# A streaming encoder trunk on one core: the first block's short rows loaded as half rows, and another order of its first casts

## The chip, the core and the metric

The kernel runs on one core of a Trainium2 chip. The time is that of the device in microseconds (us) for one execution, and the figure for a kernel is the median of its runs. Engines are named as in the profile: PE is TensorE, DVE is VectorE, ACT is ScalarE, POOL is GpSimd, and SP issues most of the transfers (DMAs).

## The reference, cut to what matters

One layer of a trunk works on 2048 prompt frames and on 32 frames of a running stream, each with 1024 channels. Everything is float32.

```python
def rmsnorm(x, g):
    y = x32 * lax.rsqrt(jnp.mean(x32 * x32, axis=-1, keepdims=True) + EPS)
    return (y * g).astype(x.dtype)

hn = rmsnorm(h, g_mix)
proj = hn @ w_in                                  # 1024 -> 3072
hA, bA, cA, zA, vB, zB = jnp.split(proj, ...)     # six bands of 512
yA = bA * (depthwise width-3 conv of cA * hA, with bias) * silu(zA)
yB = (trailing mean of vB minus vB, a linear map per group, a scale) * silu(zB)
h = h + concat[yA, yB] @ w_out
h = h + (p @ w_ple) * sigmoid(rmsnorm(h, g_ple) @ w_ple_gate)
y = rmsnorm(h, g_final)                           # also the last rows of cA*hA and vB
```

## The kernel before, in words

The frames are cut into blocks of 416 (`NB`). A block has three tiles of 128 frames and a short one of 32 rows (`DEC`). Blocks 0 and 1 form the first group. Channels lie on partitions for the products, in chunks of 128, and eight chunks make two halves of 512 channels (`NH`, `KH = 4` chunks each).

A float32 product is made of three matrix passes over numbers split in two: `hi` is the value rounded to fp32r (a cast), `lo` is the rest (a subtraction). The passes are hi·hi, hi·lo and lo·hi. `first_products` runs them for block 0 in this order for three bands at once (`zb`, `v`, `c`): the eight hi·hi matmuls of zb, of v and of c come first, then those with the frames' `lo`, then those with the weights' `lo`.

Before that, block 0 must be made ready. This is the code that is changed:

- SP loads three tiles of 128 rows (`xt_0_0`, `xt_0_1`, `xt_0_2`; below x0, x1, x2), then the short rows of blocks 0 and 1 as one tile of 64 partitions by 1024 channels (`xt_0_3`), then the raw weights of zb, v and c. SP's transfers go out in the order of its queue.
- For each tile, `x_stat` sums the squares on ACT (line 93) and makes the reciprocal root of the mean on POOL (`ms` at line 72, `rstd` at line 76). `first_normal` multiplies by it and by the gain on DVE, one half of the channels at a time (line 641). The gain lies in two PSUM banks (`gm_0`, `gm_1`, in the code `pg`).
- `first_turn` transposes on PE: four 128x128 transposes for a half of a tile, and eight 64-row transposes for the short rows (line 650). Their results are in PSUM (`pt0_0_0` is tile 0, half 0).
- `first_hi` casts from PSUM into the block's frames `B`, on ACT (one on DVE; line 663), and `first_lo` subtracts on DVE (line 667). The casts of the raw weights are at lines 694 and 712.
- `fill(n, t)` runs n transposes of the identity that nothing reads. Seven stand ahead of the first tile's transposes, then two, three and two behind those of x0, x1 and x2.

There are six PSUM banks for products (`bank`) and two others (`tbank`). The six hold `short_bank` and five of the tiles' transposes; the sixth, `pt0_2_1`, takes the bank of `pt0_0_0` when its `lo` has been made, and the first product, `zb`, takes that of `pt0_0_1`.

The order on an engine is mostly the scheduler's. What goes through `in_turn` (`tc.keep_in_program_order`) keeps the place it has in the program.

Much later the kernel loads the gate's weights with POOL's queue (line 1397). Its source is a view of four runs of 32 rows, written to a tile of 128 partitions by 512:

```python
rows = w_gate.rearrange("(q k c) n -> k q c n", q=4, k=KC)[k]
for half, t in enumerate(ts):
    ins = nc.gpsimd.dma_start(t, rows[:, :, half * NH:half * NH + NH])
```

Of the kernel before, what the change touches and what calls it, by code (L numbers as in the profile page):

```python
# [9 lines left out]
F32 = mybir.dt.float32  # L10
# [5 lines left out]
P = 128  # L16
D = 1024
# [17 lines left out]
def trunk(ctx, tc, x_p, x_s, c_conv, c_pool, p_p, p_s, g_mix, w_in, conv_w, conv_b, pool_w,  # L35
# [308 lines left out]
    with ExitStack() as s1:  # L344
# [45 lines left out]
        def fill(n, t):  # L390

            for _ in range(n):
                tc.keep_in_program_order(nc.tensor.transpose(t[:, :P], ident, ident))
# [34 lines left out]
        def turn(x, half, name, get=tbank, later=False):  # L428
            xt, n, _ = x
            pt = get(name)  # L430
            for k in range(KH):
                kk = half * KH + k
                ins = nc.tensor.transpose(pt[:, k * P:k * P + n], xt[:n, kk * P:(kk + 1) * P], ident[:n, :n])
# [167 lines left out]
        def first_products(ws):  # L601

            x = hn[0]
            out = {kind: bank(f"{kind}0_0_0") for kind in ws}
            for a, b in ((0, 0), (0, 1), (1, 0)):
                if b:
                    next(second)  # L610
                    next(second)
                for kind, w in ws.items():
                    if a:
                        if kind == "zb":
                            next(second)
                            first_los["v"]()
                        elif kind == "v":
                            first_los["c"]()
                        next(second)
                    for k in range(KC):  # L620
                        ins = nc.tensor.matmul(out[kind][:, :NB], w[k // KH][:, k % KH, a], x[k // KH][:, k % KH, b],
                                               start=a + b + k == 0, stop=a == 1 and k == KC - 1, skip_group_check=True)
                        if a + b + k or kind != "zb":
                            in_turn(ins)
# [11 lines left out]
        def first_normal(x):  # L636

            xt, m, r = x
            for half in range(2):
                h = xt[:m, half * NH:half * NH + NH]  # L640
                in_turn(nc.vector.scalar_tensor_tensor(h, h, r[:m], pg[half][:m], op0=ALU.mult, op1=ALU.mult))

        def first_turn(c, x):

            xt, m, _ = x
            if c < 3:
                return [turn(x, half, f"pt0_{c}_{half}", bank) for half in range(2)]
            t = short_bank
            for k in range(KC):
                tc.keep_in_program_order(nc.tensor.transpose(t[:, k * m:k * m + m], xt[:m, k * P:(k + 1) * P], ident[:m, :m]))  # L650
            t = t.rearrange("p (k t) -> p k t", k=KC)
            return t[:, :KH], t[:, KH:]

        first_x, turned_x = [], {}

        def place0(c, half):
            n = P if c < 3 else DEC
            piece = B0[("11", "21")[half]][:, :, :, c * P:c * P + n]
            return piece[:, :, 0], piece[:, :, 1], turned_x[c][half][:, :, :n]

        def first_hi(c, half, copy=nc.scalar.copy):
            hi, _, src = place0(c, half)
            in_turn(copy(hi, src))
# [5 lines left out]
        def first_tile(c):  # L669
            first_normal(first_x[c])  # L670
            turned_x[c] = first_turn(c, first_x[c])
            if c < 3:
                fill((2, 3, 2)[c], short_bank)


        for c in range(3):
            first_x.append(x_stat(ahead0[c], True))
        first_tile(0)
        first_hi(0, 0)
        first_x.append(x_stat(short0, True))  # L680
        short0 = first_x[3]
        first_tile(1)
        first_hi(0, 1)
        first_lo(0, 0)
        for half in range(2):
            first_hi(1, half)
        first_tile(2)
        first_hi(2, 0)
        first_tile(3)
        first_hi(2, 1, nc.vector.tensor_copy)  # L690
        raw = raw_weight("zb", 0, "firstzb")
        first_zb = [wtile(f"w_firstzb_{half}") for half in range(2)]
        for half, t in enumerate(first_zb):
            in_turn(nc.scalar.copy(t[:, :, 0], raw[:, half * KH:half * KH + KH]))
        for half in range(2):
            first_hi(3, half)
        for c in range(4):
            for half in range(2):
                if c + half:
                    first_lo(c, half)  # L700
        hn[0] = B0["11"], B0["21"]
        for half, t in enumerate(first_zb):
            nc.vector.tensor_tensor(t[:, :, 1], raw[:, half * KH:half * KH + KH], t[:, :, 0].bitcast(F32), op=ALU.subtract)
        first_w.append(first_zb)

        first_los = {}
# [13 lines left out]
            return ts  # L720

        first_w.extend(other_first(kind) for kind in ("v", "c"))
        for half in range(2):
            nc.scalar.copy(g_bc[:, half * NH:half * NH + NH], pg[half])
        B0["12"] = piece_of(seventh("B0_12"), 0)
        hn[1] = B0["12"], B0["22"]

        def second_block():

            spans = [(c, slice(c * P, min(NB, c * P + P))) for c in range(4)]  # L730
            xs = []
            for c in range(3):
                x = x_tile(f"1_{c}", [x_rows(1, c)])
                normal(x)
                xs.append((x, slice(0, P)))
                yield
            xs.append((short0, slice(DEC, 2 * DEC)))
            whole = []
            for c, cs in spans:
                x, ts = xs[c]  # L740

                turned = x[0].rearrange("p (k t) -> p k t", k=KC)[:, :, :ts.stop - ts.start]
                for half, q in enumerate(("12", "22")):
                    pt = turn(x, half, f"pt1_{c}_{half}", bank)[:, :, ts]
# [33 lines left out]
        pv = tbank("pv")  # L778
        nc.tensor.transpose(pv[:, :112], rows, ident[:112, :112])
        vec = const.tile([P, 112], F32, name="vec")  # L780
        nc.vector.tensor_copy(vec, pv[:, :112])
# [1016 lines left out]
```

## Time and profile before

| what | value |
|---|---|
| median of 3 runs | 920.51 us (919.87 to 922.76) |
| the profiled execution's own time | 922.18 us |
| its span, first to last instruction | 920.4 us |
| PE busy | 907.0 us, 99% of the span |
| DVE, ACT, POOL busy | 723.2, 482.7, 159.3 us |

The profiled execution took 1.78 us more than its span. A row of the timeline gives start, length, engine, source line, operation, output and inputs, and in brackets how long the engine was idle before and what ended that. Rows of the same kind that follow each other stand as one with a count, so the time of one is best read from the distance to the next row. A matmul's end is modelled, so its length overlaps the next one's start.

### The profile page before, as it was taken

To read this page: it belongs to the slowest core of one execution; us is meant where nothing else is said; L and a number is where in the kernel's file an instruction comes from. 1 tells how busy PE (TensorE), PEld (TensorE's weight loads), DVE (VectorE), ACT (ScalarE), POOL (GpSimd) and SP (SyncE) were. 2 spreads that over 40 slices of the span, in tenths; PEclk is the share of its full clock that TensorE was granted. 3 is DMA by queue.
4 is the path that set the end of the run, shared out by engine and by line. 5 is a ranking of instruction groups with operands and counts; after the bars stand their busy time and mean duration, and the time that the engine had idled before them with its cause. 6 is when DMAs were issued, how large, how long until landed. Compare 5 with 4: busy or idle time off the path is not lost.

```text
span 920.4 us, 13201 instructions
## 1 busy us (share of the span) xinstructions
PE 907.0 (99%) x4529; PEld 824.7 (90%) x4529; DVE 723.2 (79%) x1236; ACT 482.7 (52%) x894; POOL 159.3 (17%) x307
## 2 busy tenths in 40 slices
PE   8999999999999999999999999999999999999996
PEld 6999999999999999999999988888878878888885
DVE  6996898999576989795777579666558658889885
ACT  6744565654345555453444365444436855555554
POOL 2111222121000342310000111111113301111113
PEclk9999999999999999999999999999999999999999
DMA  8357687898945789738885468865767974576554
GB/s 247 100 141 220 170 245 230 244 282 285 416 137 172 235 231 221 231 115 303 245 243 178 146 234 278 266 218 183 237 228 230 357 262 140 206 242 231 190 201 176
DMA packets 138447, 205.12 MB, mean 223 GB/s; under 512 B 13116, under 2 KB 101724, under 8 KB 137101
## 3 DMA queue, kind: packets, MB, share of 16 engines
q1 hardware_dynamic: 117773, 139.41, 47.9%
q0 software_dynamic: 17872, 59.45, 19.6%
q10 hardware_dynamic: 2736, 5.44, 1.6%
q8 instruction: 35, 0.57, 0.3%
q14 instruction: 31, 0.25, 0.1%
HBM read 136.60 MB, written 67.64 MB: 222 GB/s over the span
## 4 chain that ended last, share of the span: by engine, by line
PE 78%; DVE 6%; DMA 3%; issue 1%; ACT 1%; POOL 0%; POOLq 0%; DVEq 0%
PE x_o L175 9%; PE x_g L175 9%; PE x_zab L593 5%; PE z_g L175 5%; PE x_zbv L593 5%; PE e L107 4%; PE z_o L175 4%; PE x_ch L593 4%; PE z_zab L593 3%; PE z_zbv L593 2%; PE z_ch L593 2%; PE y_g L175 2%; PE y_o L175 2%; PE za L593 2%; PE b L593 2%; PE h L593 1%
## 5 line engine op out<-in xcount | busy, mean ns | idle before, releaser
L80 ACT CAST y_S<-y_fS 128x512 fp32r<-128x512 f32 x32 | 19.5, 622 | 36.8 <-PE x_o L175 19.0
L175 PE MATMUL x_g<-wg_b,g_S 128*128 128x512 f32 x128 | 35.7, 390 | 0.0
L175 PE MATMUL x_o<-wo_b,y_S 128*128 128x512 f32 x128 | 35.7, 391 | 0.0
L593 PE MATMUL x_zab<-B,w_zab_S 128*128 128x416 f32 x168 | 34.2, 352 | 0.2 <-ACT V L989 0.2
L593 PE MATMUL z_zab<-B,w_zab_S 128*128 128x416 f32 x168 | 34.3, 352 | 0.0
L593 PE MATMUL x_zbv<-B,w_zbv_S 128*128 128x416 f32 x168 | 34.2, 352 | 0.0
L593 PE MATMUL z_ch<-B,w_ch_S 128*128 128x416 f32 x168 | 34.1, 352 | 0.0
L593 PE MATMUL x_ch<-B,w_ch_S 128*128 128x416 f32 x168 | 34.0, 351 | 0.0
L593 PE MATMUL z_zbv<-B,w_zbv_S 128*128 128x416 f32 x168 | 34.0, 351 | 0.0
L107 PE MATMUL e<-wq,pps 128*128 128x512 f32 x144 | 33.1, 390 | 0.0
L593 PEld LDWEIGHTS x_zab<-B,w_zab_S 128*128 128x128 f32 x168 | 31.3, 188 | 0.8 <-ACT V L989 0.5
L107 PEld LDWEIGHTS e<-wq,pps 128*128 128x128 f32 x144 | 27.0, 188 | 5.6
L593 PEld LDWEIGHTS x_ch<-B,w_ch_S 128*128 128x128 f32 x168 | 31.4, 188 | 0.3
L593 PEld LDWEIGHTS z_zbv<-B,w_zbv_S 128*128 128x128 f32 x168 | 31.4, 188 | 0.3
L593 PEld LDWEIGHTS z_ch<-B,w_ch_S 128*128 128x128 f32 x168 | 31.4, 188 | 0.3
L593 PEld LDWEIGHTS z_zab<-B,w_zab_S 128*128 128x128 f32 x168 | 31.4, 188 | 0.3
L593 PEld LDWEIGHTS x_zbv<-B,w_zbv_S 128*128 128x128 f32 x168 | 31.3, 188 | 0.4
L1343 DVE TENSOR_TENSOR c_o<-x_o,x 128x512 f32<-128x512 f32 x14 | 9.7, 691 | 26.4 <-PE x_o L175 26.4
L1566 DVE SCALAR_TENSOR_TENSOR h<-h,rstd_f,g_bc 128x1024 f32<-128x1024 f32 (+1 forms) x15 | 19.3, 1284 | 14.0 <-POOL rstd_f L76 14.0
L72 POOL TENSOR_SCALAR ms_f<-ssq_f 128x1 f32<-128x1 f32 (+1 forms) x15 | 6.6, 441 | 128.7 <-ACT junk L93 128.5
L175 PEld LDWEIGHTS x_o<-wo_b,y_S 128*128 128x128 f32 x128 | 24.0, 188 | 5.2 <-DVE c_o L1343 0.3
L175 PEld LDWEIGHTS x_g<-wg_b,g_S 128*128 128x128 f32 x128 | 24.0, 188 | 5.0
(591 smaller groups left out, 2688.5 us busy)
## 6 DMA issues: line engine op xcount, KB each, us to landing
y<-y_d SPq DMA_DIRECT2D x16, 512.0 KB, 6.7
x<-in_x_prompt_dram SPq DMA_DIRECT2D x16, 512.0 KB, 4.3
h_d<-x SPq DMA_DIRECT2D x16, 512.0 KB, 3.8
h<-h_d SPq DMA_DIRECT2D x16, 512.0 KB, 3.7
xt<-in_x_prompt_dram SPq DMA_DIRECT2D x15, 512.0 KB, 7.2
e<-e_d SPq DMA_DIRECT2D x15, 512.0 KB, 6.3
out_dram<-h POOLq DMA_DIRECT2D x14, 512.0 KB, 3.0
p_dT<-T POOLq DMA_DIRECT2D x12, 512.0 KB, 6.0
```

Source lines behind the costliest of these rows:

```text
L72: nc.gpsimd.tensor_scalar(ms[:n], ssq[:n], scalar1=1.0 / D, scalar2=EPS, op0=ALU.mult, op1=ALU.add)
L80: ins = nc.scalar.copy(hi, src)
L107: nc.tensor.matmul(ps, pps[:, a, k], wp[k][b][:, cs], start=k + q == 0, stop=k == 1 and q == 2)
L175: nc.tensor.matmul(ps[:n], lhs[:, k, a, :n], w[b][:, k], start=start and k + q == 0, stop=k == KH - 1 and q == 2, skip_group_check=True)
L593: nc.tensor.matmul(ps[:, :NB], lhs[:, k, x], b[:, k, y], start=start and k + q == 0, stop=stop and k == KH - 1 and q == 2, skip_group_chec ...
L1343: add = lambda o, a, b: nc.vector.tensor_tensor(o, a, b, op=ALU.add)
L1566: nc.vector.scalar_tensor_tensor(h[:n], h[:n], rf[:n], g_bc[:n], op0=ALU.mult, op1=ALU.mult)
```

## The change

It concerns the beginning alone, up to the first products of block 0.

- The short rows of blocks 0 and 1 (64 rows) lie as half rows on 128 partitions: partitions 0 to 63 have channels 0 to 511, partitions 64 to 127 have channels 512 to 1023. Two loads bring them, one a half. The source of each is a view of two runs of 32 rows (block, row, channel), the target 64 partitions by 512.
- These two loads now stand ahead of that of x2.
- Each partition has the squares of half a row. A product with the 0/1 matrix `pair` adds the two halves, into one column of `short_bank`. `pair` is made by two additions on DVE at the start. The mean then comes from DVE (`ms_short`, line 673) and the root from POOL.
- The fills behind the tiles (2, 3 and 2) are gone. The seven at the start stay.
- The transposes of all tiles are now pinned in the order of the program. `pt0_2_1` lies in the bank of `gm_0`, so `gm_0` is copied early to `g_bc`, and `zb` takes the bank of `pt0_0_0`.
- Casts and transposes go by halves of the channels, in an order written out by hand: short half 0, x2, short half 1, and the weights' casts between those of the frames.
- The transpose of the small vectors (`pv`) moves to a place behind the first eight matmuls of c.

The diff, cut to its core:

```diff
         short_bank = bank("pt0_3")
         fill(7, short_bank)
+        HP = P // 2
+        pair = one.tile([P, P], F32, name="pair")
+        for h in range(2):
+            nc.vector.tensor_tensor(pair[:, h * HP:h * HP + HP], ident[:, :HP], ident[:, HP:], op=ALU.add)
...
-        ahead0 = [x_load(f"0_{c}", [x_rows(0, c)]) for c in range(3)]
-        short0 = x_load("0_3", [x_rows(0, 3), x_rows(1, 3)])
+        ahead0 = [x_load(f"0_{c}", [x_rows(0, c)]) for c in range(2)]
+        short_x = ring4(xin, "xt_short")
+        for h in range(2):
+            nc.sync.dma_start(short_x[h * HP:h * HP + HP, :NH],
+                              x_p[:2 * NB, h * NH:h * NH + NH].rearrange("(b n) d -> b n d", b=2)[:, 3 * P:])
+        ahead0.append(x_load("0_2", [x_rows(0, 2)]))
...
+        def short_sums():
+            ssq = sm.tile([P, 1], F32, tag="ssq", name="ssq_short")
+            in_turn(nc.scalar.activation(junk[:, :NH], short_x[:, :NH], AF.Square, accum_out=ssq))
+            return ssq
+        def short_root(ssq):
+            in_turn(nc.tensor.matmul(short_bank[:, :1], pair, ssq, start=True, stop=True))
+            ms, r = (sm.tile([P, 1], F32, tag=t, name=f"{t}_short") for t in ("ms", "rstd"))
+            in_turn(nc.vector.tensor_scalar(ms, short_bank[:, :1], scalar1=1.0 / D, scalar2=EPS, op0=ALU.mult, op1=ALU.add))
+            nc.gpsimd.tensor_tensor(r, ms, nhalf, op=ALU.pow)
+            return r
+        def short_half(half, r):
+            hs = slice(half * HP, half * HP + HP)
+            h = short_x[hs, :NH]
+            in_turn(nc.vector.scalar_tensor_tensor(h, h, r[hs], pg[half][hs], op0=ALU.mult, op1=ALU.mult))
+            n = KH * HP
+            turned_x[3, half] = short_turn(half, short_bank[:, half * n:half * n + n], in_turn)[:, :, 0]
...
-            if c < 3:
-                fill((2, 3, 2)[c], short_bank)
...
+        for c in range(2):
+            first_x.append(x_stat(ahead0[c], True))
+        short_ssq = short_sums()
+        g_copy = lambda half: nc.scalar.copy(g_bc[:, half * NH:half * NH + NH], pg[half])
+        first_tile(0)
+        in_turn(g_copy(0))
+        first_x.append(x_stat(ahead0[2], True))
+        first_normal(first_x[1], halves=(1, 0))
+        short_r = short_root(short_ssq)
+        turned_x[1] = first_turn(1, first_x[1])
+        first_hi(0, 0)
+        first_hi(1, 0)
+        short_half(0, short_r)
+        first_normal(first_x[2], (0,))
+        first_lo(0, 0)
+        first_normal(first_x[2], (1,))
+        turned_x[2] = first_turn(2, first_x[2])
+        zb_hi(0)
+        first_hi(0, 1)
+        first_hi(3, 0)
+        first_hi(2, 0)
+        short_half(1, short_r)
+        first_hi(1, 1)
+        first_hi(2, 1, nc.vector.tensor_copy)
+        zb_hi(1)
+        first_hi(3, 1)
         for half in range(2):
-            first_hi(3, half)
-        for c in range(4):
-            for half in range(2):
+            for c in range(4):
                 if c + half:
                     first_lo(c, half)
```

How it moves instructions, at three places. The first is SP's queue, from the first tile's load to the three raw weights. Before:

```order
L412 DMA xt_0_0_171<-in_x_prompt_dram 128x1024
L412 DMA xt_0_1_173<-in_x_prompt_dram 128x1024
L412 DMA xt_0_2_175<-in_x_prompt_dram 128x1024
L412 DMA xt_0_3_177<-in_x_prompt_dram 32x1024 x2
L529 DMA raw_firstzb_267<-in_w_in_dram 128x8x128
L529 DMA raw_firstv_284<-in_w_in_dram 128x8x128
L529 DMA raw_firstc_290<-in_w_in_dram 128x8x128
```

The same stretch of SP's queue in the changed kernel:

```order
L418 DMA xt_0_0_174<-in_x_prompt_dram 128x1024
L418 DMA xt_0_1_176<-in_x_prompt_dram 128x1024
L640 DMA xt_short_178<-in_x_prompt_dram 64x1x512 x2
L418 DMA xt_0_2_181<-in_x_prompt_dram 128x1024
L535 DMA raw_firstzb_186<-in_w_in_dram 128x8x128
L535 DMA raw_firstv_282<-in_w_in_dram 128x8x128
L535 DMA raw_firstc_288<-in_w_in_dram 128x8x128
```

The short rows have gone ahead of the third tile, and each of their two loads now brings 64 half rows instead of 32 whole ones.

The second place is PE, from the first tile's transposes (`pt0_0_0`, half 0) to the first matmuls of zb. Before:

```order
L433 MATMUL pt0_0_0_203<-ident_76,xt_0_0_171 128x128 x4
L433 MATMUL pt0_0_1_208<-ident_76,xt_0_0_171 128x128 x4
L393 MATMUL pt0_3_155<-ident_76 128x128 x2
L433 MATMUL pt0_1_0_224<-ident_76,xt_0_1_173 128x128 x4
L433 MATMUL pt0_1_1_229<-ident_76,xt_0_1_173 128x128 x4
L393 MATMUL pt0_3_155<-ident_76 128x128 x3
L433 MATMUL pt0_2_0_243<-ident_76,xt_0_2_175 128x128 x4
L433 MATMUL pt0_2_1_248<-ident_76,xt_0_2_175 128x128 x4
L393 MATMUL pt0_3_155<-ident_76 128x128 x2
L650 MATMUL pt0_3_155<-ident_76,xt_0_3_177 128x64 x8
L621 MATMUL zb0_0_0_321<-B0_0_180,w_firstzb_0_269 128x416 x4
L621 MATMUL zb0_0_0_321<-B0_0_180,w_firstzb_1_270 128x416 x4
```

PE in the changed kernel:

```order
L439 MATMUL pt0_0_0_206<-ident_76,xt_0_0_174 128x128 x4
L439 MATMUL pt0_0_1_211<-ident_76,xt_0_0_174 128x128 x4
L671 MATMUL pt0_3_155<-ssq_short_202,pair_163 128x1
L439 MATMUL pt0_1_0_230<-ident_76,xt_0_1_176 128x128 x4
L439 MATMUL pt0_1_1_235<-ident_76,xt_0_1_176 128x128 x4
L662 MATMUL pt0_3_155<-ident_76,xt_short_178 128x64 x4
L439 MATMUL pt0_2_0_250<-ident_76,xt_0_2_181 128x128 x4
L439 MATMUL pt0_2_1_255<-ident_76,xt_0_2_181 128x128 x4
L662 MATMUL pt0_3_155<-ident_76,xt_short_178 128x64 x4
L628 MATMUL zb0_0_0_315<-B0_0_183,w_firstzb_0_188 128x416 x4
L628 MATMUL zb0_0_0_315<-B0_0_183,w_firstzb_1_189 128x416 x4
```

The product with `pair` stands between the transposes of x0 and x1, the fills (line 393) are gone, and the short rows' transposes stand in two parts, the second one just ahead of zb.

The third place is the way to x2's and the short rows' normalisation. On POOL, from x1's root to the first one of block 1 (`x1_0`), before:

```order
L76 TENSOR_TENSOR rstd_x0_1_193<-ms_x0_1_191,nhalf_84 128x1
L72 TENSOR_SCALAR ms_x0_2_197<-ssq_x0_2_195 128x1
L76 TENSOR_TENSOR rstd_x0_2_199<-ms_x0_2_197,nhalf_84 128x1
L72 TENSOR_SCALAR ms_x0_3_218<-ssq_x0_3_216 64x1
L76 TENSOR_TENSOR rstd_x0_3_220<-ms_x0_3_218,nhalf_84 64x1
L72 TENSOR_SCALAR ms_x1_0_352<-ssq_x1_0_350 128x1
```

POOL in the changed kernel:

```order
L76 TENSOR_TENSOR rstd_x0_1_200<-ms_x0_1_198,nhalf_84 128x1
L72 TENSOR_SCALAR ms_x0_2_219<-ssq_x0_2_217 128x1
L76 TENSOR_TENSOR rstd_x0_2_221<-ms_x0_2_219,nhalf_84 128x1
L674 TENSOR_TENSOR rstd_short_227<-ms_short_226,nhalf_84 128x1
L72 TENSOR_SCALAR ms_x1_0_349<-ssq_x1_0_347 128x1
```

DVE in the changed kernel, from x1's normalisation to the first `lo` behind the cast of `pt0_2_1`:

```order
L652 SCALAR_TENSOR_TENSOR xt_0_1_176<-xt_0_1_176,rstd_x0_1_200,gm_0_151 128x512
L673 TENSOR_SCALAR ms_short_226<-pt0_3_155 128x1
L680 SCALAR_TENSOR_TENSOR xt_short_178<-xt_short_178,rstd_short_227,gm_0_151 64x512
L652 SCALAR_TENSOR_TENSOR xt_0_2_181<-xt_0_2_181,rstd_x0_2_221,gm_0_151 128x512
L698 TENSOR_TENSOR B0_0_183<-pt0_0_0_206,B0_0_183 128x4x128
L652 SCALAR_TENSOR_TENSOR xt_0_2_181<-xt_0_2_181,rstd_x0_2_221,gm_1_152 128x512
L680 SCALAR_TENSOR_TENSOR xt_short_178<-xt_short_178,rstd_short_227,gm_1_152 64x512
L694 CAST B0_0_183<-pt0_2_1_255 128x4x128
L698 TENSOR_TENSOR B0_0_183<-pt0_1_0_230,B0_0_183 128x4x128
```

On POOL the short rows' root still comes behind x2's, while on DVE the short rows' first half now comes ahead of x2's normalisation.

More of the change, by code (lines that the diff above doesn't have):

```diff
@@ L609, in first_products @@
                 if b:
+                    vectors()
                     next(second)
@@ L634, in in_turn, with first_normal @@
             tc.keep_in_program_order(ins)
-        def first_normal(x):
+        def first_normal(x, halves=(0, 1)):
             xt, m, r = x
-            for half in range(2):
+            for half in halves:
                 h = xt[:m, half * NH:half * NH + NH]
@@ L643, in first_turn, with short_turn @@
         def first_turn(c, x):
-            xt, m, _ = x
-            if c < 3:
[L647 to L652, printed above, removed]
+            gets = (bank, tbank if c == 2 else bank)
+            return [turn(x, half, f"pt0_{c}_{half}", gets[half], True) for half in range(2)]
+        def short_turn(half, t, pin=lambda ins: None):
+            hs = slice(half * HP, half * HP + HP)
+            for k in range(KH):
+                pin(nc.tensor.transpose(t[:, k * HP:k * HP + HP], short_x[hs, k * P:k * P + P], ident[hs, hs]))
+            return t.rearrange("p (k b t) -> p k b t", k=KH, b=2)
+        def short_sums():
[9 more added lines that the diff above has]
+        def short_half(half, r):
+            hs = slice(half * HP, half * HP + HP)
+            h = short_x[hs, :NH]
+            in_turn(nc.vector.scalar_tensor_tensor(h, h, r[hs], pg[half][hs], op0=ALU.mult, op1=ALU.mult))
+            n = KH * HP
+            turned_x[3, half] = short_turn(half, short_bank[:, half * n:half * n + n], in_turn)[:, :, 0]
         first_x, turned_x = [], {}
@@ L671, in first_tile, with zb_hi @@
             turned_x[c] = first_turn(c, first_x[c])
-            if c < 3:
-                fill((2, 3, 2)[c], short_bank)
[L676 to L690, printed above, removed]
         raw = raw_weight("zb", 0, "firstzb")
         first_zb = [wtile(f"w_firstzb_{half}") for half in range(2)]
-        for half, t in enumerate(first_zb):
-            in_turn(nc.scalar.copy(t[:, :, 0], raw[:, half * KH:half * KH + KH]))
+        def zb_hi(half, copy=nc.scalar.copy):
+            in_turn(copy(first_zb[half][:, :, 0], raw[:, half * KH:half * KH + KH]))
+        for c in range(2):
[24 more added lines that the diff above has]
+        first_hi(3, 1)
         for half in range(2):
-            first_hi(3, half)
-        for c in range(4):
-            for half in range(2):
+            for c in range(4):
                 if c + half:
@@ L702, in trunk @@
         for half, t in enumerate(first_zb):
-            nc.vector.tensor_tensor(t[:, :, 1], raw[:, half * KH:half * KH + KH], t[:, :, 0].bitcast(F32), op=ALU.subtract)
+            in_turn(nc.vector.tensor_tensor(t[:, :, 1], raw[:, half * KH:half * KH + KH], t[:, :, 0].bitcast(F32), op=ALU.subtract))
         first_w.append(first_zb)
@@ L722, in trunk @@
         first_w.extend(other_first(kind) for kind in ("v", "c"))
-        for half in range(2):
-            nc.scalar.copy(g_bc[:, half * NH:half * NH + NH], pg[half])
+        g_copy(1)
         B0["12"] = piece_of(seventh("B0_12"), 0)
@@ L777, in trunk, with vectors @@
         nc.sync.dma_start(rows[100:108].rearrange("k (q c) -> k q c", q=4), g_ple[0].rearrange("(q k c) -> k q c", q=4, k=KC))
-        pv = tbank("pv")
-        nc.tensor.transpose(pv[:, :112], rows, ident[:112, :112])
         vec = const.tile([P, 112], F32, name="vec")
-        nc.vector.tensor_copy(vec, pv[:, :112])
+        def vectors():
+            pv = tbank("pv")
+            nc.tensor.transpose(pv[:, :112], rows, ident[:112, :112])
+            nc.vector.tensor_copy(vec, pv[:, :112])
         cw = lambda r, j: vec[:, r * 4 + j:r * 4 + j + 1]
```

15 lines of the change are left out of this document (9 added, 6 removed).

## The prediction

> **What bounds the kernel now.** I read the page first, then the timeline of the first 27 us by engine, since the change ends there.
>
> ```profile
> span 920.4 us, 13201 instructions
> PE 907.0 (99%) x4529; PEld 824.7 (90%) x4529; DVE 723.2 (79%) x1236; ACT 482.7 (52%) x894; POOL 159.3 (17%) x307
> PE 78%; DVE 6%; DMA 3%; issue 1%; ACT 1%; POOL 0%; POOLq 0%; DVEq 0%
> ```
>
> PE is busy for 907.0 of 920.4 us, and the chain that ended last is PE's for 78%. A later start of PE's products is therefore paid in full, unless a gap behind it shrinks. The place to look is the first product.
>
> ```profile
> 5.93 1.75 PE L393 MATMUL pt<-ident 128*128 128x128 f32 x7
> 7.48 1.92 PE L433 MATMUL pt<-ident,xt 128*128 128x128 f32 x8
> 9.19 0.63 PE L393 MATMUL pt<-ident 128*128 128x128 f32 x2
> 9.61 1.91 PE L433 MATMUL pt<-ident,xt 128*128 128x128 f32 x8
> 12.74 1.38 PE L433 MATMUL pt<-ident,xt 128*128 128x128 f32 x8 [0.68 <-DVE xt L641]
> 14.26 0.93 PE L650 MATMUL pt<-ident,xt 64*128 64x64 f32 x8
> 16.02 1.75 PE L621 MATMUL zb<-B,w_firstzb 128*128 128x416 f32 x8 [0.83 <-DVE B L667]
> 17.61 1.67 PE L621 MATMUL v<-B,w_firstv 128*128 128x416 f32 x8
> 25.30 1.03 PE L433 MATMUL pt<-ident,xt 128*128 128x128 f32 x8
> ```
>
> The products start at 16.02 and then run without a gap. Eight transposes took 1.92 us at 7.48 and 1.03 us at 25.30: PE ran at about half speed at first.
>
> ```profile
> 28.00:32.00 4.00, 3.83 (x27) 3.53 (x26) 3.28 (x6) 4.00 (x9) 0.00 (x0) 1.00 0.49 130
> 32.00:36.00 4.00, 3.78 (x25) 3.17 (x24) 4.00 (x11) 4.00 (x12) 0.00 (x0) 1.00 0.00 0
> ```
>
> In these windows of busy times PE (first sum behind the comma) idles 0.39 us in 8 us, waiting for ACT and DVE. Those start later by as much, so the gaps give nothing back.
>
> What leads to 16.02 is x2's load, and behind it a chain over ACT, POOL, DVE and PE:
>
> ```profile
> 5.90 1.06 ACT L93 ACTIVATE junk<-xt 128x1024 bf16<-128x1024 f32 x1 [0.35 <-DMA xt<-in_x_prompt_dram]
> 9.68 1.06 ACT L93 ACTIVATE junk<-xt 128x1024 bf16<-128x1024 f32 x1 [2.64 <-DMA xt<-in_x_prompt_dram]
> 10.65 0.19 ACT L93 ACTIVATION_READ_ACCUMULATOR junk<-xt 128x1 f32 x1
> 14.15 1.15 ACT L694 CAST w_firstzb<-raw_firstzb 128x512 fp32r<-128x512 f32 x2
> ```
>
> ```profile
> 10.92 0.19 POOL L72 TENSOR_SCALAR ms_x<-ssq_x 128x1 f32<-128x1 f32 x1 [2.96 <-ACT junk L93]
> 11.19 0.55 POOL L76 TENSOR_TENSOR rstd_x<-ms_x,nhalf 128x1 f32<-128x1 f32 x1
> ```
>
> ```profile
> 6.49 2.91 DVE L641 SCALAR_TENSOR_TENSOR xt<-xt,rstd_x,gm 128x512 f32<-128x512 f32 x4 [4.30 <-POOL rstd_x L76]
> 11.34 0.69 DVE L667 TENSOR_TENSOR B<-pt,B 128x512 fp32r<-128x512 f32 x1 [1.94 <-ACT B L663]
> 11.94 2.73 DVE L641 SCALAR_TENSOR_TENSOR xt<-xt,rstd_x,gm 128x512 f32<-128x512 f32 x4
> ```
>
> x1 was there at 5.90 and x2 at 9.68, each when ACT's wait for the load ended. From x2's squares to its root is 9.68 to 11.74, 2.06 us. On DVE four normalisations take 2.73 us, 0.68 each, and a subtraction 0.60 (11.34 to 11.94).
>
> **The change: the two new loads.** Each brings 64 half rows, 131 KB, from a source view of two runs of 32 rows. The trace has no such load on SP's queue, so I bound it by two others. The tiles' loads, of 128 rows each, use all 16 DMA engines. The gate's weights are loaded by POOL's queue from a view of four runs of 32 rows, two loads of 256 KB at a time:
>
> ```profile
> 2.20:3.60 1.40, 1.34 (x2) 0.83 (x3) 0.00 (x0) 0.03 (x1) 0.25 (x1) 1.00 0.97 366
> 7.00:10.00 3.00, 3.00 (x16) 3.00 (x15) 2.30 (x4) 0.36 (x2) 0.74 (x2) 1.00 1.12 184
> 10.50:14.00 3.50, 2.73 (x17) 2.23 (x16) 2.66 (x5) 3.50 (x9) 1.46 (x4) 1.00 1.21 289
> 638.80:639.60 0.80, 0.80 (x5) 0.65 (x4) 0.77 (x2) 0.00 (x0) 0.00 (x0) 1.00 0.24 82
> ```
>
> ```profile
> 633.61 1.42 POOL L1397 DMA_DIRECT2D gs<-in_w_ple_gate_dram  x2 [6.53 <-DMA g_d<-gs]
> ```
>
> The last two numbers of a window are the DMA engines' busy share and GB/s. The tiles came at 366 GB/s with a share of 0.97, 23 GB/s an engine. The end of the gate's weights (issued at 633.61), with one load left, came at 82 GB/s with a share of 0.24: four of 16 engines, 20.5 GB/s each. A view of four runs was carried by four engines, so I expect two engines for two runs. The 262 KB of both loads then take 262/41 = 6.4 us at 20.5 GB/s an engine, or 262/46 = 5.7 us at 23, if both use the same two. The lower end is all 16 engines: 262/366 = 0.7 us. I take 6.0, since the gate's load has the same form, and I see no reason in SP's rows for the second load to go elsewhere; both ends are kept for the range.
>
> [...]
>
> So the short rows land at 5.90 + 6.0 = 11.9. x2 is queued behind them on those two engines and needs its usual 524/366 = 1.4 us there: 13.3 instead of 9.68. The raw weights follow at 289 GB/s, 1.8 us each: zb at 15.1, v at 16.9, c at 18.7. In the new order ACT casts them at about 15.5 (zb), 18.5 (v) and 19.5 (c), so these stay off the path; in the trace of before zb's cast followed at 14.15 without a wait.
>
> **The chain behind x2.** ACT does the short rows' squares (half of 1.06, and 0.19) from 11.9 and `gm_0`'s copy while x2 is coming, at no cost. x2's root is ready at 13.3 + 2.06 = 15.4. The short rows' root is queued behind it on POOL: +0.55, 15.9. DVE's next instruction is the short rows' first half, and behind it wait x2's first half, a `lo`, x2's second half and the short rows' second half: 4 x 0.68 + 0.60 = 3.3, to 19.2. PE then has four short transposes ahead of zb, half of 0.93: 19.7. The last casts of zb's second half (0.2 to 0.6 us on ACT and DVE) lie beside zb's first four matmuls, 0.8 us. The first product comes at 19.7 instead of 16.02: +3.7.
>
> Small parts: the `pair` additions lie in DVE's 4.30 us of idling ahead of 6.49; without that they would cost two short additions. The product with `pair` and `ms_short` cost some 0.5 us while PE and DVE wait for x2 anyway. `zb` no longer waits for a `lo` (0.83 us at 16.02), but what it now waits for is later. The `pv` transpose only changes place. SP issues as many loads ahead of the weights as before.
>
> **PE's speed.** Before, PE worked without a pause from 5.93 (fills, transposes, fills) and was fast by 12.74. Now x1's transposes stand behind the product with `pair`, which waits for the short rows: PE idles from about 9.4 to 12.7. It resumes with gaps: x1 at 12.8, the short half at 16.7, x2 at 17.4. If it must be kept busy as long as before (from 5.93 to about 11.8, 5.9 us, first to fast), it is fast at 16.7 + 5.9 = 22.6, and the 2.9 us from 19.7 run at 1.03/1.92 of the speed: 1.3 us lost. The lower end is 0 (fast at once, as x1's transposes count too); the upper is a full 5.9 us from 19.7, 2.7. I take 1.0, near the 1.3.
>
> [...]
>
> **The sum.** 3.7 + 1.0 = +4.7. The profiled execution took 922.18 (span 920.4 and 1.78 around it), which would become 926.9. That execution lies 1.67 above the median of 920.51; for the median I predict 925.2.
>
> **Rivals.**
> - [...] Chance 0.14.
> - *The loads use two different pairs of engines*: 3.2 us, x2 at 10.5, or later by the 2.4 us that it was late before (it was due at 5.90 + 1.4 = 7.3 and came at 9.68): the product moves by +0.9 to +3.3, and with 0.6 for the speed 923.2. For it: POOL's two loads did overlap. Chance 0.10, half of it over 0.3%.
> - *The slow stretch hits the two engines too.* From 7 to 10 us the loads moved 184 GB/s, half the usual, and made x2 2.4 us late. If the short rows lose as much, 927.6. Chance 0.11.
> - *No change (the other side)*: the short rows spread over 16 engines as the tiles do. Then x2 is at 5.9 + 0.7 + 1.4 + 2.4 = 10.4, the chain of 6.4 us ends at 16.8, +0.8, and PE hardly pauses: 921.3. It decides if the two loads take less than 4.0 us together, since each us of them is one of the sum and 2.8 of the 4.7 mark the border. Against it stands the gate's 82 GB/s. Chance 0.12.
> - *Faster*: as the last, but x2 without its lateness, at 8.0: the product at 14.4, 1.6 earlier, 918.9. The order by halves gives no more, as zb's weights were cast at 14.15. Chance 0.05, with 0.02 beyond 0.3%.
>
> **How the numbers follow.** The main case has 0.48: loads of 5.7 to 6.4 us and 0.6 to 1.7 us for the speed give 924.5 to 926.3, and the speed's upper end 927.3. About 0.3% (2.8 us, below 917.7 or above 923.3) is what a measurement can tell from no change. Slower: 0.48 + 0.14 + 0.05 + 0.11 = 0.78. Same: 0.05 + 0.12 + 0.03 = 0.20. Faster: 0.02. The range of 921.2 to 927.4 leaves out the faster case, half of the slow stretch and a part of the no-change case, under 0.2.
>
> **What would show it.** ACT's squares of the short rows begin at about 11.9 and those of x2 at about 13.3, both after a wait for a DMA; at 7 and 10 the load term is wrong. PE idles some 3 us ahead of the product with `pair`. The windows from 6 to 10 us show the same total GB/s with two engines behind the others. The first zb matmul stands near 19.7, and eight hi·hi matmuls there take more than the 1.6 us between 16.02 and 17.61; at the same distance the speed term is wrong. Behind the first products nothing changes by more than 0.3 us; a large gap there would be a cost that I have missed.

## The result and the profile after

The changed kernel takes 929.62 us (median; 928.84 to 931.75), the kernel before 920.29 us on the same chip (919.75 to 922.76). The ratio is 1.0102, with a 95% interval of 1.0084 to 1.0119: 9.3 us slower. 925.2 was predicted, within 921.2 to 927.4; 929.62 lies above that. The sign was right, the size was half of what came.

The profiled execution took 930.58 us. The page of the changed kernel: its span, the busy times, the chain that ended last.

```profile
span 928.8 us, 13191 instructions
PE 909.6 (98%) x4524; PEld 825.2 (89%) x4524; DVE 723.1 (78%) x1239; ACT 482.6 (52%) x894; POOL 159.1 (17%) x306
PE 85%; DVE 6%; DMA 5%; ACT 2%; issue 1%; SPq 1%; POOL 0%; POOLq 0%; DVEq 0%; ACTq 0%
```

The span grew by 8.4 us, PE's busy time only by 2.6. DMA went from 3% to 5% of the chain. The place is again the start; the timeline of PE after (start, duration, engine, line, tiles, count, and in brackets what it waited for):

```profile
7.78 1.97 PE L439 MATMUL pt<-ident,xt 128*128 128x128 f32 x8
14.10 0.59 PE L671 MATMUL pt<-ssq_short,pair 128*128 128x1 f32 x2 [4.35 <-ACT junk L667]
15.35 1.97 PE L439 MATMUL pt<-ident,xt 128*128 128x128 f32 x8 [0.67 <-DVE xt L652]
17.89 0.69 PE L662 MATMUL pt<-ident,xt_short 64*128 64x64 f32 x4 [0.57 <-DVE xt_short L680]
18.55 2.37 PE L439 MATMUL pt<-ident,xt 128*128 128x128 f32 x8
20.85 0.69 PE L662 MATMUL pt<-ident,xt_short 64*128 64x64 f32 x4
21.47 3.14 PE L628 MATMUL zb<-B,w_firstzb 128*128 128x416 f32 x8
24.40 2.11 PE L628 MATMUL v<-B,w_firstv 128*128 128x416 f32 x8
27.88 1.76 PE L628 MATMUL zb<-B,w_firstzb 128*128 128x416 f32 x8
32.52 1.03 PE L439 MATMUL pt<-ident,xt 128*128 128x128 f32 x8
```

The first product stands at 21.47 instead of 16.02. Eight matmuls of zb take 3.14 us there and 1.76 us at 27.88; eight transposes take 1.97 us at 15.35 and 1.03 us at 32.52. PE ran at about half speed until 25.3, where the trace's first clock record, at full speed, begins. The second zb pass starts at 27.88, 7.13 us later than in the kernel before, whose row is:

```profile
20.75 1.68 PE L621 MATMUL zb<-B,w_firstzb 128*128 128x416 f32 x8
```

ScalarE's timeline after: x1's squares, the short rows', x2's.

```profile
6.23 1.06 ACT L93 ACTIVATE junk<-xt 128x1024 bf16<-128x1024 f32 x1 [0.20 <-DMA xt<-in_x_prompt_dram]
13.32 0.63 ACT L667 ACTIVATE junk<-xt_short 128x512 bf16<-128x512 f32 x1 [5.94 <-DMA xt_short<-in_x_prompt_dram]
14.49 1.06 ACT L93 ACTIVATE junk<-xt 128x1024 bf16<-128x1024 f32 x1
```

The short rows came at 13.32 (11.9 predicted), and x2's squares start at 14.49 (13.3 predicted, 9.68 before). The trace's landing records show, besides one right behind each issue (3.09 and 3.65), two completions for each short load: at 9.28 and 9.97, and at 12.56 and 13.22. Of x2's 16 parts 14 had landed by 8.6, the other two at 13.70 and 14.40, behind the short loads. Windows of busy times after (the last three columns are PE's clock, the DMA engines' share and GB/s; the clock column shows 1.00 where no record has come yet, so for the speed in these two windows only the lengths above count):

```profile
7.00:10.00 3.00, 2.75 (x12) 2.02 (x11) 2.07 (x3) 0.38 (x2) 0.74 (x2) 1.00 0.93 228
12.50:14.50 2.00, 0.40 (x2) 0.41 (x2) 0.00 (x0) 1.18 (x4) 0.00 (x0) 1.00 0.14 45
```

At the end about two engines work alone, as an estimate from the second window: a share of 0.14 is 2.2 of 16, and 45 GB/s is about 22 for each of two.

**The loss in three terms.** From x2's squares to the first product it was 6.34 us before (9.68 to 16.02) and is 6.98 after (14.49 to 21.47). From the first product to the second zb pass it was 4.72 and is 6.41. So 7.13 = 4.81 (x2 later) + 0.64 (a longer chain) + 1.69 (slow first passes).

### The profile page after: what moved, and what is told of

Read it like the earlier page. It is cut to its first block, busy times and chain, and to the rows that moved or that the text cites. A ratio compares the mean times of both kernels' runs of the same rounds, so it can differ in the third digit from the quotient of the medians.

```text
span 928.8 us, 13191 instructions
## 1 busy us (share of the span) xinstructions
PE 909.6 (98%) x4524; PEld 825.2 (89%) x4524; DVE 723.1 (78%) x1239; ACT 482.6 (52%) x894; POOL 159.1 (17%) x306
## 4 chain that ended last, share of the span: by engine, by line
PE 85%; DVE 6%; DMA 5%; ACT 2%; issue 1%; SPq 1%; POOL 0%; POOLq 0%; DVEq 0%; ACTq 0%
PE x_o L175 9%; PE x_g L175 9%; PE x_zab L599 6%; PE x_zbv L599 5%; PE z_g L175 5%; PE e L107 4%; PE z_o L175 4%; PE x_ch L599 4%; PE z_zbv L599 3%; PE za L599 3%; PE z_zab L599 3%; PE b L599 3%; PE h L599 2%; PE z_ch L599 2%; PE y_g L175 2%; PE y_o L175 2%
```

## The experiments

All times are medians; the ratio is to the kernel before, run beside it on the same chip.

**1. The short rows by loads of one run each**, nothing else undone:

```diff
-            nc.sync.dma_start(short_x[h * HP:h * HP + HP, :NH],
-                              x_p[:2 * NB, h * NH:h * NH + NH].rearrange("(b n) d -> b n d", b=2)[:, 3 * P:])
+            for b in range(2):
+                at, r = h * HP + b * DEC, b * NB + 3 * P
+                nc.sync.dma_start(short_x[at:at + DEC, :NH], x_p[r:r + DEC, h * NH:h * NH + NH])
```

> The changed kernel with one thing undone: the short half rows come by four loads of 32 rows x 512 from one run of rows each, in place of two loads from a view of two runs. Place in the queue, halves and order stay as changed. Theory 'two engines' (the loads' form costs most): the short rows land before 9 us, x2 at 9.5 to 10.5, the first product stands at 16 to 17.5 instead of 21.5, and the time is 920.5 to 923. Rival 'order' (the halves of the channels, the product with pair and the longer chain cost it, whatever carries the loads): the first product stays behind 19 and the time is at least 926.

922.43 us, ratio 1.0013 (1.0004 to 1.0021). Its timeline, ScalarE and PE:

```profile
7.35 0.63 ACT L668 ACTIVATE junk<-xt_short 128x512 bf16<-128x512 f32 x1
8.65 1.06 ACT L93 ACTIVATE junk<-xt 128x1024 bf16<-128x1024 f32 x1
15.63 3.14 PE L628 MATMUL zb<-B,w_firstzb 128*128 128x416 f32 x8
18.57 1.83 PE L628 MATMUL v<-B,w_firstv 128*128 128x416 f32 x8
```

Neither square waits for a load any more. The first product comes 5.84 us earlier than in the changed kernel, and even 0.39 earlier than before. So halves, `pair` and order don't cost the 9 us; the form of two loads does. What is left is the slow clock (3.14 us for zb's pass): the second zb pass comes at 21.78, still 1.03 us later than before.

**2. The converse: the two-run load put into the kernel before.**

```diff
-        short0 = x_load("0_3", [x_rows(0, 3), x_rows(1, 3)])
+        short0 = (ring4(xin, "xt_0_3"), 2 * DEC, "x0_3")
+        nc.sync.dma_start(short0[0][:2 * DEC], x_p[:2 * NB].rearrange("(b n) d -> b n d", b=2)[:, 3 * P:])
+        ahead0.append(x_load("0_2", [x_rows(0, 2)]))
```

(The first line of `ahead0` loads two tiles instead of three, so that x2 stands behind.)

> The kernel before with one part of the change alone: both short loads are replaced by one load of 64 whole rows (262 KB) from the view of two runs, ahead of x2's load. No halves, no product with pair, the old order, the fills kept. Theory 'two engines': x2 lands at 13.5 to 14.5 instead of 9.7, the first product stands at 19.8 to 20.8 instead of 16.0, the time is 924.5 to 927. Rival 'order': the first product stays before 17.5 and the time is 919.5 to 922.

929.21 us, ratio 1.0087 (1.0074 to 1.0100): this part alone makes nearly the whole loss. It is more than expected, since x2 came later than I thought (15.04, at most 14.5 expected) and PE lost its full speed in the longer wait (clock record at 15.96). ScalarE (x1, x2) and PE:

```profile
6.27 1.06 ACT L93 ACTIVATE junk<-xt 128x1024 bf16<-128x1024 f32 x1 [0.73 <-DMA xt<-in_x_prompt_dram]
15.04 1.06 ACT L93 ACTIVATE junk<-xt 128x1024 bf16<-128x1024 f32 x1 [7.62 <-DMA xt<-in_x_prompt_dram]
21.89 3.14 PE L621 MATMUL zb<-B,w_firstzb 128*128 128x416 f32 x8 [0.35 <-ACT B L665]
```

**3. Half of the cost: one two-run load, the other half of the channels by two loads of one run.**

```diff
+            if h:
                 nc.sync.dma_start(short_x[h * HP:h * HP + HP, :NH], ...)
+                continue
+            for b in range(2): ...
```

> The changed kernel with half of the suspected cost: the first half of the channels comes by two loads from one run of rows each, the second half still by one load from the view of two runs (131 KB). Theory 'two engines' (the bytes that two engines carry set the start, about 3.4 us for each load): the short rows land near 10 instead of 13.2, x2 at 10.8 to 11.5 instead of 14.4, the first product stands at 17.8 to 18.7 instead of 21.5, half way to that of the spread loads (15.6), and the time is about 3.3 us over that kernel's 922.4: 925 to 926.5. Rival 'a view of two runs is late whatever it carries': first product at 20 or later, time 928 or more.

926.22 us, ratio 1.0055 (1.0042 to 1.0068): the time is in the expected range, the first product (19.59) is later than expected. One load costs more than half of two. In the trace the spread loads had landed by 6.70, the two-run load at 11.41: 4.7 us for 131 KB on two engines. In the next experiment such a load takes 3.0 us (8.2 to 11.21, behind x2). The windows show one thing that differs, the traffic of the other engines (ScalarE and PE of this kernel first, then its window, then that of experiment 4):

```profile
11.52 0.63 ACT L672 ACTIVATE junk<-xt_short 128x512 bf16<-128x512 f32 x1 [4.33 <-DMA xt_short<-in_x_prompt_dram]
12.62 1.06 ACT L93 ACTIVATE junk<-xt 128x1024 bf16<-128x1024 f32 x1
19.59 3.14 PE L628 MATMUL zb<-B,w_firstzb 128*128 128x416 f32 x8
```

```profile
6.70:11.40 4.70, 2.84 (x14) 2.44 (x12) 2.06 (x3) 0.49 (x2) 0.74 (x2) 1.00 1.15 244
```

```profile
8.20:11.20 3.00, 1.05 (x6) 0.81 (x5) 0.44 (x1) 0.00 (x0) 0.00 (x0) 1.00 0.45 135
```

The mean busy share of the 16 engines was 1.15 in the first and 0.45 in the second. One packet of a half row (2 KB) took 142 ns on average in experiment 3 (7 to 10 us) and 96 ns in experiment 4 (8 to 10 us).

**4. x2's load ahead of the short loads.**

```diff
-        ahead0 = [x_load(f"0_{c}", [x_rows(0, c)]) for c in range(2)]
+        ahead0 = [x_load(f"0_{c}", [x_rows(0, c)]) for c in range(3)]
...
-        ahead0.append(x_load("0_2", [x_rows(0, 2)]))
```

> The changed kernel with x2's load ahead of the two short loads in SP's queue; the short loads keep their form. Theory 'two engines work their queue off in order, and whoever stands last is late': x2 lands before 10 instead of 14.4, the short rows at 14.0 to 14.6 instead of 13.2. ScalarE's order is kept, short rows first, so the chain starts 1 us later: first product at 22 to 22.8 instead of 21.5, time 930 to 931. Rival 'only x2's lateness behind the short rows costs': the first product comes 1 us earlier or more, time 928.5 or less.

928.89 us, ratio 1.0082 (1.0069 to 1.0095). The rows are as expected: x2 landed by 8.2, the short rows at 14.26, the first product at 22.43, 0.96 later than in the changed kernel. Here the order in the queue only decided who was late. x2 lay ready from 8.2, but ScalarE still took the short rows first; x2 first on ScalarE too wasn't tried. The time is under the 930 that I expected: behind 119 us the distance to the kernel before shrinks by 2.0 us in the traces (below).

```profile
14.36 0.63 ACT L666 ACTIVATE junk<-xt_short 128x512 bf16<-128x512 f32 x1 [7.41 <-DMA xt_short<-in_x_prompt_dram]
15.45 1.06 ACT L93 ACTIVATE junk<-xt 128x1024 bf16<-128x1024 f32 x1
22.43 3.14 PE L628 MATMUL zb<-B,w_firstzb 128*128 128x416 f32 x8
```

Experiments 1, 3 and 4 and the changed kernel differ only in these loads. Their first products come 6.98, 6.97, 6.98 and 6.98 us behind the start of x2's squares (8.65, 12.62, 15.45, 14.49). In these four, each us by which the loads delayed x2's squares delayed the first product by the same.

**5. TensorE kept busy in the changed kernel.**

```diff
         first_tile(0)
+        fill(24, short_bank)
...
+        fill(8, short_bank[:, KH * HP:])
         turned_x[1] = first_turn(1, first_x[1])
+        ahead_bank = bank("pt0_2_0")
+        fill(10, ahead_bank)
```

> The changed kernel with TensorE kept busy while it waits: 24 extra transposes behind x0's, 8 behind the product with pair, 10 ahead of the first short half, none of whose results is used. Theory 'clock' (the idling ahead of the product with pair makes the first products run slow): the first passes of zb and v take 1.6 and 1.5 us instead of 2.9 and 2.0, the transposes just before take half as long, the second zb pass comes 1.8 to 2.4 us earlier, the time is 927.2 to 928. Rival 'transposes don't count for the clock': the same durations as in the changed kernel, 929.3 to 930.

929.68 us, ratio 1.0094 (1.0081 to 1.0107). The passes did get faster, and the second zb pass came 1.17 us earlier (26.71), less than expected, since the extra transposes also delayed x2's (first product 21.75). By 40 us the lead is gone (7.46 us behind the kernel before, against 7.13 in the changed kernel): with the extra instructions the second block's copies and casts stand in another order on ScalarE, and PE waits 1.34 us for one of them at 35.59. The time is the one that the rival gave, but for another reason.

```profile
21.75 2.10 PE L628 MATMUL zb<-B,w_firstzb 128*128 128x416 f32 x8
23.69 1.67 PE L628 MATMUL v<-B,w_firstv 128*128 128x416 f32 x8
35.59 0.66 PE L439 MATMUL pt<-ident,xt 128*128 128x128 f32 x4 [1.34 <-ACT xt L792]
```

Its windows (PE's clock is the third number from the end):

```profile
9.80:16.60 6.80, 4.32 (x38) 4.00 (x37) 0.81 (x2) 2.82 (x6) 0.83 (x3) 1.00 0.59 161
16.63:20.03 3.40, 3.40 (x18) 3.07 (x17) 2.94 (x5) 1.59 (x3) 0.40 (x1) 0.50 0.47 131
20.04:26.00 5.96, 5.89 (x38) 5.21 (x38) 5.04 (x10) 5.64 (x12) 0.00 (x0) 1.00 0.76 272
```

PE was fast in the 24 transposes from 9.46 (2.95 us for all of them). The records have half speed from 16.62, after the pauses around the product with `pair`, to 20.03, and full speed then, behind 3.4 us of transposes without a pause and ahead of any product of zb, v or c.

**6. The kernel before without its extra transposes between the tiles.**

```diff
-            if c < 3:
-                fill((2, 3, 2)[c], short_bank)
```

> The kernel before without the seven extra transposes between its tiles (2, 3 and 2; their results were never used). Theory 'clock': TensorE is at full speed later, the first passes of zb and v take longer, the second zb pass comes 0.5 to 1.5 us later, the time is 921 to 922. Rival 'transposes don't count, or the others are enough': no row changes by more than 0.2 us, 920.0 to 920.6.

923.74 us, ratio 1.0031 (1.0019 to 1.0043). The first product comes 0.26 us earlier, the passes are slow, and the second zb pass is 1.45 us later (22.20), as the clock theory had it; the time lost 0.6 us more than that (923.74 against 921.68 beside it).

```profile
15.76 3.11 PE L621 MATMUL zb<-B,w_firstzb 128*128 128x416 f32 x8 [0.43 <-ACT B L663]
18.67 2.07 PE L621 MATMUL v<-B,w_firstv 128*128 128x416 f32 x8
```

**7. Spread loads, and the short rows' root ahead of x2's on GpSimd.** On top of experiment 1:

```diff
-        first_x.append(x_stat(ahead0[2], True))
         first_normal(first_x[1], halves=(1, 0))
         short_r = short_root(short_ssq)
+        first_x.append(x_stat(ahead0[2], True))
```

> The kernel with the spread loads (four of one run each), and the short rows' root on GpSimd ahead of the root of x2 instead of behind it. Theory: the short rows' first half no longer waits for x2, 0.6 us earlier on VectorE, so TensorE goes without a pause from its seven first transposes to the first product; that comes at 14.9 to 15.4 instead of 15.6 and at full speed (zb's pass 1.6 to 2.3 us instead of 2.9). Time 919.5 to 921.5, 1 to 2.5 us under the spread loads alone. Rival: the chain over x2 sets the product, nothing moves by more than 0.3 us, time 922 to 923.

920.03 us, ratio 0.9989 (0.9980 to 0.9997): slightly faster than the kernel before (921.08 beside it), and so than the changed one. The root moved from 10.68 to 9.97 and the first product to 14.94, as expected; PE was fast by 10.5 but slow again from 13.9 (the short rows' four transposes took 0.46 us at 11.35 and 0.66 at 14.35), so zb's pass took 2.86, more than expected. The profiled execution took 922.77 us, the longest of the twelve, so this slow pass need not be there in the others.

```profile
9.97 0.55 POOL L675 TENSOR_TENSOR rstd_short<-ms_short,nhalf 128x1 f32<-128x1 f32 x1 [1.92 <-DVE ms_short L674]
14.94 2.86 PE L628 MATMUL zb<-B,w_firstzb 128*128 128x416 f32 x8
```

**8. Spread loads, and four extra transposes in PE's pauses** (on top of experiment 1):

```diff
         turned_x[1] = first_turn(1, first_x[1])
+        ahead_bank = bank("pt0_2_0")
+        fill(2, ahead_bank)
...
+                one_half = turn(x, 0, "pt0_2_0", lambda name: ahead_bank, True)
+                next_bank = tbank("pt0_2_1")
+                fill(2, next_bank)
+                return [one_half, turn(x, 1, "pt0_2_1", lambda name: next_bank, True)]
```

> The kernel with the spread loads, and four extra transposes whose results are not used: two behind x1's, two between the halves of x2's. Theory 'clock' (pauses of 0.3 to 0.4 us in TensorE's row of transposes are what keeps the first products slow there): zb's first pass takes 1.6 to 2.2 us instead of 2.9 and the second zb pass comes 0.8 to 1.5 us earlier than with the spread loads alone (21.8), time 920.5 to 921.8. Rival 'such short pauses don't matter': the passes stay at 2.9 and 1.8 and the four transposes cost up to 0.4 us, 922.4 to 923.

920.31 us, ratio 0.9990 (0.9982 to 0.9999), also slightly faster than the kernel before (921.08). The second zb pass comes at 19.57, 2.21 us earlier than with the spread loads alone: more than expected, since the transposes are fast too (four of x2's took 0.66 us at 12.47). But the trace's clock record has full speed from 9.94 (the eight transposes from 9.51 took 1.28 us, 1.97 with the spread loads alone), ahead of the first extra transposes (10.63), so in this execution they can have kept it, not won it; how much of the 2.21 us is theirs isn't shown.

```profile
10.63 0.38 PE L393 MATMUL pt<-ident 128*128 128x128 f32 x2
14.91 1.78 PE L628 MATMUL zb<-B,w_firstzb 128*128 128x416 f32 x8
```

**9. Both together.**

> The spread loads, the short rows' root ahead of x2's, and the four extra transposes together. Theory: both gains add, first product at 14.2 to 14.7 (15.6 with the spread loads alone, 14.9 with either of the two), zb's first pass at full speed (1.6 to 1.9 us), second zb pass at 18.9 to 19.4; time 918.8 to 920.2, 1.0 to 2.2 us under the kernel before. Rival: the later start is already hidden, since ScalarE and VectorE must cast x2's second half and the short rows first; first product at 14.8 or later, time as with either alone, 920 to 920.5.

920.65 us, ratio 0.9999 (0.9989 to 1.0009): no sum of the two can be seen; the time lies just above the rival's range. In its profile the passes are fast, but x1 came late (its squares start at 6.89, 5.96 in experiment 8), and the first product stands at 15.28. Counted from x1's squares that is 8.39 us, against 8.95 in both single variants. Whether the two gains add stays open.

```profile
6.89 1.06 ACT L93 ACTIVATE junk<-xt 128x1024 bf16<-128x1024 f32 x1 [0.95 <-DMA xt<-in_x_prompt_dram]
15.28 1.78 PE L628 MATMUL zb<-B,w_firstzb 128*128 128x416 f32 x8
```

**10. The changed kernel once more.**

> The changed kernel once more, unchanged, beside the others on one chip. Theory 'the start costs 7.4 us and the rest of the 9.3 us is how the waits behind 119 us fell in the first runs': 7.5 to 8.8 us over the kernel before, and TensorE's wait for the cast at about 160 us is 0.2 to 1.2 us long instead of 1.7. Rival 'the change also lengthens that wait': 9 to 10 us over the kernel before, and the wait is 1.5 us or more again.

929.40 us, ratio 1.0090 (1.0074 to 1.0106), 8.3 us over the kernel before. In this profile v's first pass is already fast, and the second zb pass comes at 27.02, 6.27 us later than before. Its timeline and windows:

```profile
21.30 2.83 PE L628 MATMUL zb<-B,w_firstzb 128*128 128x416 f32 x8
23.97 1.68 PE L628 MATMUL v<-B,w_firstv 128*128 128x416 f32 x8
```

```profile
10.00:13.30 3.30, 0.00 (x0) 0.00 (x0) 0.00 (x0) 0.07 (x1) 0.00 (x0) 1.00 0.71 150
13.40:23.60 10.20, 8.29 (x33) 6.71 (x34) 7.00 (x13) 8.47 (x19) 1.25 (x3) 0.50 0.64 200
23.70:30.00 6.30, 6.30 (x36) 6.20 (x35) 5.80 (x10) 4.03 (x8) 4.08 (x6) 1.00 0.62 194
```

PE's clock fell to half at 13.4, while PE waited for the short rows, and was back only at 23.6, though PE worked from 15.3 with short pauses (0.50 us the longest). The same program was fast at 23.6 here and at 25.3 in its first profile, and from the first product to the second zb pass it took 5.72 us here and 6.41 there. So 0.9 us of the start (27.88 against 27.02) differs between two executions of one program.

The wait near 160 us was to tell the theories apart. PE's longest waits there (us in total, times, longest) were, in the first profile of the changed kernel and in this one:

```profile
PE pt_g L439 <- DVE 11_1_1_1640 L83: 1.7, 1, 1.7
```

```profile
PE pt_g L439 <- DVE 11_1_1_1640 L83: 1.3, 1, 1.3
```

1.3 lies between what the two theories gave. The same wait was 1.1 us before and 0.3 in experiments 4, 8 and 9, so it doesn't follow how late the start is.

## Why the prediction was wrong in size

**The loads: right in kind, 1.1 us too short.** The step "I expect two engines for two runs" held: two completions a load, where x2 has 16, one load after the other (9.28 and 9.97, then 12.56 and 13.22), and the windows' 45 GB/s at a share of 0.14. Experiments 1 and 2, which take the form away and add it alone, show that it is the cause. The term that failed is the 6.0 us. From x1 to the short rows it took 7.1 (6.23 to 13.32) and 6.9 in experiment 10. I had two rates, 23 GB/s an engine for the tiles and 20.5 for the gate's weights, and used them for the stretch from 7 to 10 us, which the kernel before already shows to be slow: 184 GB/s at a share of 1.12, 11.5 an engine. In experiment 4, where the other engines had less to do (shares of 0.45 and 0.49), the rates hold: 131 KB in 3.0 us, 22 GB/s an engine, and 6.06 us for both loads. At the share of 1.15 the same bytes took 4.7 us (experiment 3). In all x2's squares came 1.19 us later than predicted: 1.09 from the loads and 0.33 since x1 itself came later (6.23, not 5.90), less 0.23 since they followed the short rows by 1.17 us, not 1.4. The rival "the slow stretch hits the two engines too" named this, with a chance of 0.11; it was a part of the answer.

**The chain behind x2: 0.58 us too short.** DVE did what was said (from x2's squares to the end of the short rows' second half 6.0 us, 5.9 predicted). But I put four fast transposes behind it, 0.47 us; PE was at half speed and still had x2's second half to do, 0.94 us from 20.53 to 21.47. The slow clock was counted on the products and forgotten on the transposes ahead of them.

**The clock: 1.69, and 1.00 in experiment 10, for 1.0.** The step "if it must be kept busy as long as before, 5.9 us, first to fast" was the wrong picture: it gave full speed at 22.6, and the records have 25.34 and, in experiment 10, 23.6. That the second execution loses just the predicted 1.0 us is luck. Where the windows show both ends of a stretch at half speed, it lasted 3.41 us (experiment 5, 16.62 to 20.03), 6.83 (experiment 6, 12.72 to 19.55), 10.24 (experiment 2, 15.96 to 26.20) and 10.2 (experiment 10, 13.4 to 23.6). How much work brings full speed isn't settled by them: in experiment 5 PE worked through its 3.41 us (3.40 of 3.40 us), in experiment 6 for 6.34 of 6.77 us and was slow all the while, and in the changed kernel it was still slow 3.87 us into the products (21.47 to 25.34), which run without a pause. That PE would be slow was right: the chance of 0.14 stood for a PE that is fast when the products start, and no run of the changed kernel shows that, since zb's first pass took 3.14 us and 2.83 in experiment 10. So was the reading that transposes count: full speed came at 11.82 us in the kernel before and at 20.03 in experiment 5, each time behind transposes alone, which PE did without a pause in the 3.4 us ahead of it.

**"Behind the first products nothing changes by more than 0.3 us": wrong.** Of the 8.39 us by which PE's last products end later in the first profile, 1.26 come behind the second zb pass; 0.66 of it is the wait near 160 us, 1.73 instead of 1.07 us. In experiment 10's profile only 0.2 us come behind it, so this is no fixed cost of the change. Behind about 119 us all kernels of the record issue the same instructions in the same order, and still the distance to the kernel before changes there, from -2.0 us (experiment 4) to +1.1 us (experiment 6), with no order by how late the start is. What sets the waits there, at about 160 us above all, wasn't found.

**What was right.** x2's squares follow the short rows; the product with `pair` and `ms_short` cost nothing; the raw weights stay off the path; PE pauses ahead of the product with `pair`, 4.35 us instead of 3. One wait was not foreseen and harmless: DVE did x1's first half only at 14.55, behind ScalarE's copy of `gm_0` from the same bank.

```profile
14.55 0.75 DVE L652 SCALAR_TENSOR_TENSOR xt<-xt,rstd_x,gm 128x512 f32<-128x512 f32 x1 [5.47 <-ACT g_bc L714]
```

Together the three terms of the start were short by 1.19, 0.58 and 0.69 us: 2.46 of the 4.6 between 4.7 and 9.3. The rest lies behind them: 1.26 in later waits and 0.93 in how the two profiled runs stand to their medians (1.89 above for the kernel before, 0.96 for the changed one). The prediction had carried the distance of before's profiled run to its median over to the changed kernel. In experiment 10 the start is short by only 1.6 us (1.02, 0.58 and 0.00) of the 3.6 between 4.7 and 8.3; 0.2 are later waits and 1.8 the profiled runs' distances to their medians. So the loads and the chain were short in both executions, and the rest of the miss varies from one to the other.

## What to carry over

A load from a view of two runs had two completions here, and a share of 0.14, which is 2.2 of 16 engines, at its end; x2's load had 16 completions. Count the engines that carry a load in a trace before moving it to the front of a queue: two parts of x2, which stood behind it, landed only at 13.70 and 14.40, the other 14 by 8.6. Four plain loads beat two elegant ones here, 922.4 against 929.6 us. Take the rate for a load from the stretch in which it will run (131 KB took 3.0 us in one and 4.7 in another). Where PE waits at the start, work that is thrown away can keep it fast (without it the kernel before lost 2 us, experiment 6), but look at what the extra instructions do to the order of everything behind them.

## What the runs showed of the hardware

- The same bytes took two engines over half as long again: 131 KB took 3.0 us at a share of 0.45 (experiment 4) and 4.7 us at 1.15 (experiment 3). The share alone isn't the cause: in the kernel before, the tiles' packets (4 KB) took 171 to 177 ns from 2 to 5 us, at a share of 0.97 (2.2 to 3.6 us), and 268 to 347 ns from 7 to 10 us, at 1.12, beside the raw weights' packets of 512 bytes. What slows them there wasn't tried by itself.
- How long a pause takes PE's full speed isn't settled by these traces: its clock fell to half 5.15 us after the last work in experiment 2 (10.81 to 15.96), and 2.4 us after it in experiment 6 (10.30 to 12.72), where PE had begun again at 12.46.
- SP's queue stood still at times, and the next load was issued only behind that. In the changed kernel the issue of two raw weights takes 4.60 and 5.49 us, to 14.36; in the kernel before one takes 5.75 us, to 10.53, and in experiment 1 2.28 us, to 8.37. What SP waits for isn't shown. The rows of the changed kernel, then that of before:

```profile
4.22 4.60 SPq L535 DMA_DIRECT2D raw_firstv<-in_w_in_dram  x1
8.87 5.49 SPq L535 DMA_DIRECT2D raw_firstc<-in_w_in_dram  x1
```

```profile
4.78 5.75 SPq L529 DMA_DIRECT2D raw_firstc<-in_w_in_dram  x1
```
